# Fourteen modulation sums moved from an output projection to the projections ahead of it, pieces of a step issued in written order, and attention's values read as alternating streams

## The chip, the core and the metric

The kernel runs on one core of a Trainium2 chip. The metric is the device time in microseconds (us) of one execution; less is better. Each kernel is one launch that reads its inputs from device memory (HBM) and writes its output there.

## The reference, cut to what matters

The reference is a decoder trunk of two layers on 512 tokens of width 2048, in fp32. Layer 0 mixes tokens by chunkwise retention with 8 heads, layer 1 by multi-head latent attention with 16 heads. Each layer is modulated by a vector c through a matrix product of its own, and the last lines below are what the moved sums and the values belong to.

```python
c_act = jax.nn.silu(c)
for i in range(DEPTH):                                   # 2 layers
    mod = (c_act @ ada_w[i] + ada_b[i])[:, None, :]      # 2048 -> 3 * 2048
    shift, scale, gate = jnp.split(mod, 3, axis=-1)
    h = rmsnorm(x, norm_g[i]) * (1.0 + scale) + shift
    y = retention_branch(h, ...) if i == 0 else mla_branch(h, ...)
    x = x + gate * y
return rmsnorm(x, final_norm_g)

# retention_branch: proj = h @ w_in (q, k, v, g); rope on q and k; 4 chunks of 128 tokens;
#                   group norm; (silu(g) * y) @ w_out
# mla_branch:       proj = h @ w_in (cq, ckv, k_rope, g); q and k, v from the low ranks; rope;
s = jnp.where(key_pos[None, :] <= qpos[:, None], s, -1e30)
p = jax.nn.softmax(s, axis=-1)
o = jnp.einsum('bhqk,bhkd->bhqd', p, v)                  # the values
#                   (silu(g) * o) @ w_out
```

## The kernel before, in words

Every fp32 matrix product is done on TensorE (PE) as three products of parts: an operand is split into a high part (a cast on ScalarE, ACT) and a low part (the rest, a subtraction on VectorE, DVE), and `mm3` adds high by high, high by low and low by high into one PSUM bank. A weight tile so passes through four hands before PE can finish with it: a DMA brings it, DVE forms sums of its blocks (many projections are done with seven block products in place of eight, which `seven_steps` and `seven_rows_steps` write), ACT casts the high part, DVE makes the low part.

The work is a list of steps. A step has `prepare` (the sums and splits of its weights, on DVE and ACT), `multiply` (on PE), `follow` (what its results need), and pieces of other work that are put beside it (`step.beside["form"]` and others), such as the splits of the rope tables or a head's decayed scores. The step loop issues them in order. A list scheduler then orders the instructions of each engine by their due times; `behind(V_, A_)` around a block says that what is issued in it goes behind what stood there on DVE (`V_`) and ACT (`A_`), so that inside one block the scheduler may reorder and between blocks it may not.

The stages, in order of time: the modulation of layer 0 and the first norm (to about 150 us); the projections of layer 0 (to about 800 us), where heads alternate between `heads_steps(h)` (values and gate, tiles `vg_...`) and `qk_steps(h)` (queries and keys of a head, tiles `qk_...`); the output projection of layer 0 with the retention itself beside it (to about 1370 us, called o1 here, in three rounds of 16 steps, `round_steps`); the input projections of layer 1, among them the gate `g` and the shared rotary key `kr` (to about 1500 us); attention with its up-projections (to about 1890 us); the last output projection.

The modulation of later use (the gate of layer 0 and all of layer 1) isn't done on PE: `later_modulation` loads a 128x1024 piece of the matrix (0.52 MB) and DVE multiplies it with c and sums it in one instruction (tile `mod`, L1194). There are 96 such sums. A step's `rows` says how many of them are fetched with it; they run on DVE a step or two later. `light(block, ...)` gives the numbers of the steps of an o1 round that get one.

Two ways of reading a moving operand occur. `mm3` by default reads with `paired`: elements 0, n/2, 1, n/2+1, ... that is, two streams in turn. The values of attention (`values`, a head's 12 products of 512, 384, 256 and 128 columns) read straight through, with `read=lambda t: t`.

Names that come up again: `x_qk, s_qk, z_qk, y_qk` and `x, s, z, y` are PSUM accumulators of the seven-product scheme; `qk_01e` and `qk_01o` are the even and odd weight tiles of the second step of a `qk_steps`, and `_r` marks the raw tile. `m` are the results of the scheme that DVE adds up at the end of a head. In o1, `o_p` are split weights, `o_h, o_l` the parts of the gated results `yT` (L1369, transposed on PE), `s_0f` to `s_3f` the decayed scores (L1317), `rope_t` the rope (L1265 to L1267). In the gate's stage `h_f` and `sums_f` (L514 to L519) are sums of blocks of the activations, `kr_sum` (L1812) the sum of the two halves of the rotary key, and `kr_sw` its swapped quarters (four copies on ACT, L1818).

## Time and profile before

| what | number |
|---|---|
| median of three runs | 2047.1 us (2046.78 to 2047.33) |
| the profiled execution's own time | 2047.42 us |
| its span | 2045.6 us |
| mean granted TensorE clock | 0.999 of full speed |
| matmuls, share of the span in which PE was busy | 11124, 99% |
| DVE busy | 82% |
| ACT busy | 51% |
| HBM traffic | 418 MB read, 43 MB written |

The span is what the profiler sees of the program on the core; 1.8 us of the execution's own time lie outside of it. A busy engine in the table is one with an instruction in it. PE's matmuls overlap one another, so how much time PE lost is read from the distance between the starts of matmuls, not from the busy share.

### The profile page before, as it was taken

What the parts mean: (1) busy time and instruction counts of PE and PEld (TensorE: products, weight loads), DVE (VectorE), ACT (ScalarE), POOL (GpSimd) and SP (SyncE); (2) the same over time, 40 slices, a digit from 0 to 9 for tenths busy, and PEclk for the clock granted to TensorE, in tenths of its full rate; (3) what the DMA queues carried; (4) which work ended last, traced back from release to release, by engine and by line L of the source; (5) the groups of instructions that cost most, each with busy time, mean ns of one, the idle gap of its engine ahead of it and who ended that gap; (6) DMA issues with size and microseconds to landing.
All of it is one profiled execution on the core that took longest, in us unless ns stands there. A gap on an engine that the chain in (4) does not pass through costs nothing.

```text
span 2045.6 us, 30080 instructions
## 1 busy us (share of the span) xinstructions
PE 2020.9 (99%) x11124; PEld 1807.7 (88%) x11124; DVE 1673.8 (82%) x2506; ACT 1051.9 (51%) x1622; POOL 103.6 (5%) x176
## 2 busy tenths in 40 slices
PE   8999999999999999999999999999999999999998
PEld 6888898999999888888888888899889999999888
DVE  7999888888889889766777878778988788887765
ACT  6765444545454544434444445445446676674444
POOL 1001000000000000000000000010000000000000
PEclk9999999999999999999999999999999999999999
DMA  9985887878787778865757656753467644346644
GB/s 382 406 309 170 274 293 223 288 234 271 254 272 257 240 250 294 267 199 188 243 176 240 223 190 241 273 189 114 160 206 214 199 144 148 120 151 220 232 152 144
DMA packets 230101, 462.95 MB, mean 226 GB/s; under 512 B 20881, under 2 KB 84401, under 8 KB 226369
## 3 DMA queue, kind: packets, MB, share of 16 engines
q1 hardware_dynamic: 217312, 421.07, 62.1%
q0 software_dynamic: 11920, 38.91, 4.9%
q8 instruction: 87, 1.43, 0.3%
q10 hardware_dynamic: 722, 1.06, 0.2%
q14 instruction: 60, 0.49, 0.1%
HBM read 417.96 MB, written 43.00 MB: 225 GB/s over the span
## 4 chain that ended last, share of the span: by engine, by line
PE 72%; DVE 14%; ACT 5%; DMA 5%; issue 3%; SPq 0%; POOL 0%; DVEq 0%; ACTq 0%; POOLq 0%
PE o L1512 5%; PE o L2487 4%; PE x L907 2%; PE s L908 2%; PE s L906 2%; PE y L906 2%; PE y L908 2%; PE x L908 2%; PE y L907 2%; PE s L907 2%; PE x L906 2%; PE x_qk L1007 2%; PE uv L2076 2%; PE s_qk L1007 2%; PE y_qk L1007 2%
## 5 line engine op out<-in xcount | busy, mean ns | idle before, releaser
L1512 PE MATMUL o<-o_h,o_p 128*128 128x512 f32 (+1 forms) x1088 | 311.6, 368 | 0.2 <-DVE o_p L136 0.2
L1512 PEld LDWEIGHTS o<-o_h,o_p 128*128 128x128 f32 x1088 | 201.0, 189 | 25.9 <-DVE o_p L136 0.6
L1512 PE MATMUL o<-o_l,o_p 128*128 128x512 f32 (+1 forms) x544 | 199.8, 367 | 0.4 <-DVE o_l L1390 0.4
L1512 PEld LDWEIGHTS o<-o_l,o_p 128*128 128x128 f32 x544 | 103.0, 189 | 13.7 <-DVE o_l L1390 1.2
L136 DVE TENSOR_TENSOR o_p<-o_r,o_p 128x1024 fp32r<-128x1024 f32 x64 | 78.1, 1222 | 45.1 <-ACT o_p L135 45.1
L2487 PE MATMUL o<-o_h,o_w 128*128 128x512 f32 (+1 forms) x336 | 79.8, 330 | 0.0
L1194 DVE SCALAR_TENSOR_TENSOR mod<-mod,c_odd 128x1024 f32<-128x1024 f32 x56 | 67.3, 1220 | 14.6 <-DMA mod<-in_ada_t_dram 14.6
L135 ACT CAST o_p<-o_r 128x1024 fp32r<-128x1024 f32 x64 | 66.5, 1050 | 17.4 <-DMA o_r<-in_ret_w_out_dram 9.1
L412 DVE SCALAR_TENSOR_TENSOR aw<-aw,c_all 128x2048 f32<-128x2048 f32 (+1 forms) x37 | 73.2, 1997 | 2.0 <-DMA aw<-in_ada_t_dram 2.0
L181 PE MATMUL qk<-hT,qk_p 128*128 128x512 f32 x192 | 73.1, 381 | 1.2 <-ACT g_st L497 1.2
L183 PE MATMUL qk<-hT,qk_p 128*128 128x512 f32 x192 | 73.1, 380 | 0.4 <-DVE qk_p L136 0.4
L182 PE MATMUL qk<-hT,qk_p 128*128 128x512 f32 x192 | 72.8, 379 | 0.0
L2487 PEld LDWEIGHTS o<-o_h,o_w 128*128 128x128 f32 x336 | 57.8, 190 | 4.7
L1356 ACT ACTIVATE yn<-y,nmr,gn_r 128x512 f32<-128x512 f32 x32 | 22.3, 778 | 66.8 <-DVE nmr L1350 66.8
L2487 PE MATMUL o<-o_l,o_w 128*128 128x512 f32 (+1 forms) x168 | 55.4, 329 | 0.0
L135 ACT CAST o_h<-o_in 128x1024 fp32r<-128x1024 f32 x24 | 25.1, 1047 | 55.7 <-PE o L182 36.9
L136 DVE TENSOR_TENSOR o_l<-o_in,o_h 128x1024 fp32r<-128x1024 f32 x24 | 29.3, 1222 | 28.4 <-ACT o_h L135 28.4
L1194 DVE SCALAR_TENSOR_TENSOR mod<-mod,c_bm 128x1024 f32<-128x1024 f32 x40 | 48.7, 1219 | 0.0
L181 PE MATMUL o<-o_h,o_w 128*128 128x512 f32 x128 | 48.7, 381 | 0.0
L182 PE MATMUL o<-o_l,o_w 128*128 128x512 f32 x128 | 48.5, 379 | 0.0
L183 PE MATMUL o<-o_h,o_w 128*128 128x512 f32 x128 | 48.5, 379 | 0.0
L136 DVE TENSOR_TENSOR o_w<-o_w_raw,o_w 128x1024 fp32r<-128x1024 f32 x32 | 38.8, 1219 | 8.5 <-ACT o_w L135 8.4
(1533 smaller groups left out, 6194.4 us busy)
## 6 DMA issues: line engine op xcount, KB each, us to landing
mod<-in_ada_t_dram SPq DMA_DIRECT2D x96, 512.0 KB, 5.7
o_r<-in_ret_w_out_dram SPq DMA_DIRECT2D x64, 512.0 KB, 5.5
aw<-in_ada_t_dram SPq DMA_DIRECT2D x28, 1024.0 KB, 9.7
mod_gate<-in_ada_t_dram SPq DMA_DIRECT2D x32, 512.0 KB, 4.8
o_w_raw<-in_mla_w_out_dram SPq DMA_DIRECT2D x32, 512.0 KB, 4.5
qk_r<-in_ret_w_in_dram SPq DMA_DIRECT2D x48, 256.0 KB, 3.6
qk_r<-qk_d SPq DMA_DIRECT2D x32, 256.0 KB, 6.0
v_r<-v_d SPq DMA_DIRECT2D x32, 256.0 KB, 5.7
```

The lines of the kernel that those rows point to most:

```text
L135: ACT.copy(hi, src)
L136: DVE.tensor_sub(lo, src, hi.bitcast(F32))
L181: PE.matmul(o, lhs[0], read(rhs[0]), start=first and not seeded, stop=False, skip_group_check=seeded)
L182: PE.matmul(o, lhs[0], read(rhs[1]), start=False, stop=False, skip_group_check=seeded)
L183: return PE.matmul(o, lhs[1], read(rhs[0]), start=False, stop=last, skip_group_check=seeded)
L906: PE.matmul(banks[b], a[0], paired(w[0]), start=first, stop=False, skip_group_check=True)
L907: PE.matmul(banks[b], a[0], paired(w[1]), start=False, stop=False, skip_group_check=True)
L908: PE.matmul(banks[b], a[1], paired(w[0]), start=False, stop=True, skip_group_check=True)
L1007: PE.matmul(o, w[wp][:, i, b * P : (b + 1) * P], paired(a[ap]), start=first and i + b + k == 0, stop=k == 2, skip_group_check=True,)
L1194: DVE.scalar_tensor_tensor(out=aw, in0=aw, scalar=1.0, in1=silu_c[j], op0=ALU.mult, op1=ALU.mult, accum_out=row_sums[piece][:, j, b : b + 1],)
L1512: PE.matmul(o, w[i][:, ki, c0 + b * P : c0 + (b + 1) * P], read(a[j]), start=first and i + j == 0, stop=last and i == 1, skip_group_check= ...
L2487: PE.matmul(banks2[b][:, cols], w[0][i][:, 0, b * P : (b + 1) * P], read(o2_moving(w, u, cols)[j]), start=u + i + j == 0, stop=u == KD - 1 ...
```

## The change

It has four parts. (1) Three views are new: `paired_blocks` reads each 128-column block as two streams of 64 in turn, `turned_blocks` and `folded_blocks` undo that in the result. (2) The numbers of sums per step change: in the second half of each head's seven-product steps (`heads_steps`) every step but the first and the last gets one, in `qk_steps` three steps instead of two; that places 14 more sums in the projections. The three o1 rounds get 11, 11 and 12 sums in place of 16 each. (3) `values` reads with `paired_blocks`, and the multiplication that follows reads the result in the turned way. (4) Each piece of `step.beside["form"]` now stands in a block of its own, so that the pieces of a step keep their written order on DVE and ACT.

```diff
+    def paired_blocks(t):
+        return t.rearrange("p (b a n) -> p b n a", a=2, n=P // 2)
+
+    def turned_blocks(t):
+        return t.rearrange("p (b n a) -> p b a n", a=2, n=P // 2)
+
+    def folded_blocks(t):
+        return t.rearrange("p (b a n) -> p b a n", a=2, n=P // 2)
...
-            lambda second, u: int(second and (u % 2 == 1 or (h > 5 and u in (2, 4)))),
+            lambda second, u: int(second and 0 < u < 7),
...
-            f"qk{h}", load_half, hT, sums1, *turns1, finish, lambda second, u: int(second and u < 2),
+            f"qk{h}", load_half, hT, sums1, *turns1, finish, lambda second, u: int(second and u < 3),
...
-        light(block, (0, 0, 2, 3, 4, 6, 6, 7, 9, 9, 11, 11, 12, 13, 13, 15))
+        light(block, (0, 0, 2, 3, 4, 6, 6, 7, 9, 12, 15) + ((13,) if n == 2 else ()))
...
-                    (pt[j][:, 0, o : o + w], pt[j][:, 1, o : o + w]), m == 0, m == NT - 1, read=lambda t: t,
+                    (pt[j][:, 0, o : o + w], pt[j][:, 1, o : o + w]), m == 0, m == NT - 1, read=paired_blocks,
...
-            DVE.tensor_mul(o2, side["o"], side["sg"])
+            DVE.tensor_mul(folded_blocks(o2), turned_blocks(side["o"]), folded_blocks(side["sg"]))
...
-        with behind(V_, A_):
-            for form_ in step.beside["form"]:
+        for form_ in step.beside["form"]:
+            with behind(V_, A_):
                 form_()
```

The change adds nine lines ahead of most of the code, so that L1044 of before is L1053 of the changed kernel.

The first place is DVE where head 1 ends and the `qk_steps` of head 2 begin (tiles `qk_00`, `qk_01`; `m_1_...` are the four results of head 1). Before:

```order
L1044 TENSOR_TENSOR qk_00e<-qk_00e_r,qk_00e 128x1024
L1047 TENSOR_TENSOR qk_00o<-qk_00o_r,qk_00o 128x1024
L1104 TENSOR_TENSOR m_1_0_2162<-m_1_0_2162,y_0_1831 128x512
L1106 TENSOR_TENSOR m_1_0_2120<-m_1_0_2120,y_0_1831 128x512
L1104 TENSOR_TENSOR m_1_1_2164<-m_1_1_2164,y_1_1832 128x512
L1106 TENSOR_TENSOR m_1_1_2122<-m_1_1_2122,y_1_1832 128x512
L1040 TENSOR_TENSOR qk_01e_r<-qk_01e_r 128x2x256
L1042 TENSOR_TENSOR qk_01o_r<-qk_01o_r,qk_01e_r 128x2x256
L1043 TENSOR_TENSOR qk_01o_r<-qk_01o_r 128x2x256
L1044 TENSOR_TENSOR qk_01e<-qk_01e_r,qk_01e 128x1024
L1047 TENSOR_TENSOR qk_01o<-qk_01o_r,qk_01o 128x1024
L1194 SCALAR_TENSOR_TENSOR mod_2_0_11_2351,mod_2_0_c<-mod_2_0_11_2351,c_bm_2156 128x1024
```

And in the changed kernel:

```order
L1053 TENSOR_TENSOR qk_00e<-qk_00e_r,qk_00e 128x1024
L1056 TENSOR_TENSOR qk_00o<-qk_00o_r,qk_00o 128x1024
L1203 SCALAR_TENSOR_TENSOR mod_2_0_21_2325,mod_2_0_c<-mod_2_0_21_2325,c_bm_2156 128x1024
L1113 TENSOR_TENSOR m_1_0_2162<-m_1_0_2162,y_0_1831 128x512
L1115 TENSOR_TENSOR m_1_0_2120<-m_1_0_2120,y_0_1831 128x512
L1113 TENSOR_TENSOR m_1_1_2164<-m_1_1_2164,y_1_1832 128x512
L1115 TENSOR_TENSOR m_1_1_2122<-m_1_1_2122,y_1_1832 128x512
L1049 TENSOR_TENSOR qk_01e_r<-qk_01e_r 128x2x256
L1051 TENSOR_TENSOR qk_01o_r<-qk_01o_r,qk_01e_r 128x2x256
L1052 TENSOR_TENSOR qk_01o_r<-qk_01o_r 128x2x256
L1053 TENSOR_TENSOR qk_01e<-qk_01e_r,qk_01e 128x1024
L1056 TENSOR_TENSOR qk_01o<-qk_01o_r,qk_01o 128x1024
```

A sum now stands ahead of the four results and of the tiles of the second step, and the one behind `qk_01o` is gone from there. On PE, at the second step of the same `qk_steps`, before:

```order
L1007 MATMUL x_qk_2423<-hT_537,qk_01e 128x256 x6
L1007 MATMUL x_qk_2423<-hT_674,qk_01e 128x256 x6
L1007 MATMUL s_qk_2424<-sums_1510,qk_01e 128x256 x6
L1007 MATMUL s_qk_2424<-sums_1555,qk_01e 128x256 x6
L1007 MATMUL z_qk_2425<-hT_554,qk_01o 128x256 x6
```

And in the changed kernel:

```order
L1016 MATMUL x_qk_2430<-hT_537,qk_01e 128x256 x2
L1016 MATMUL s_qk_2431<-sums_1510,qk_01e 128x256 x2
L1016 MATMUL z_qk_2432<-hT_554,qk_01o 128x256
L1016 MATMUL x_qk_2430<-hT_537,qk_01e 128x256 x4
L1016 MATMUL x_qk_2430<-hT_674,qk_01e 128x256 x6
L1016 MATMUL s_qk_2431<-sums_1510,qk_01e 128x256 x4
```

Three products, two of `s_qk` and one of `z_qk`, now stand between the first two of `x_qk` and the third, which is the first that reads the low part of `qk_01e`.

The second place is DVE in an o1 round, where the rope of the next head and the low parts of the gated results meet. Before:

```order
L136 TENSOR_TENSOR o_2_0_2_p<-o_2_0_2_r,o_2_0_2_p 128x1024
L1265 TENSOR_TENSOR rope_0_0_t_10789<-qk_6_r,cos_7826 128x512
L1266 TENSOR_TENSOR rope_0_0_t_10790<-qk_6_r,sin_7828 128x512
L1267 TENSOR_TENSOR rope_0_0_t_10789<-rope_0_0_t_10789,rope_0_0_t_10790 128x512
L1390 SCALAR_TENSOR_TENSOR o_l_0_10777<-yT_0_10749,vcol,o_h_0_10776 128x512
L1390 SCALAR_TENSOR_TENSOR o_l_0_10777<-yT_1_10754,vcol,o_h_0_10776 128x512
L1390 SCALAR_TENSOR_TENSOR o_l_2_10779<-yT_2_10759,vcol,o_h_2_10778 128x512
L1390 SCALAR_TENSOR_TENSOR o_l_2_10779<-yT_3_10764,vcol,o_h_2_10778 128x512
L136 TENSOR_TENSOR qk_0_0p<-rope_0_0_t_10789,qk_0_0p 128x512
```

And in the changed kernel:

```order
L136 TENSOR_TENSOR o_2_0_2_p<-o_2_0_2_r,o_2_0_2_p 128x1024
L1399 SCALAR_TENSOR_TENSOR o_l_0_10789<-yT_0_10761,vcol,o_h_0_10788 128x512
L1399 SCALAR_TENSOR_TENSOR o_l_0_10789<-yT_1_10766,vcol,o_h_0_10788 128x512
L1399 SCALAR_TENSOR_TENSOR o_l_2_10791<-yT_2_10771,vcol,o_h_2_10790 128x512
L1399 SCALAR_TENSOR_TENSOR o_l_2_10791<-yT_3_10776,vcol,o_h_2_10790 128x512
L1274 TENSOR_TENSOR rope_0_0_t_10801<-qk_6_r,cos_7872 128x512
L1275 TENSOR_TENSOR rope_0_0_t_10802<-qk_6_r,sin_7874 128x512
L1276 TENSOR_TENSOR rope_0_0_t_10801<-rope_0_0_t_10801,rope_0_0_t_10802 128x512
L136 TENSOR_TENSOR qk_0_0p<-rope_0_0_t_10801,qk_0_0p 128x512
```

The four low parts moved ahead of the three instructions of the rope.

The third place is DVE in the gate's stage of layer 1, where the rotary key's sum and the activations' sums meet (`g_1_0_p`, `g_1_1_p` are the gate's split weights). Before:

```order
L136 TENSOR_TENSOR g_1_0_p<-g_1_0_r,g_1_0_p 128x1024
L514 TENSOR_TENSOR h_f<-h_2_12499 128x512
L514 TENSOR_TENSOR h_f<-h_3_12503 128x512
L1812 TENSOR_TENSOR kr_sum<-kr_ps,kr_other 128x512
L516 TENSOR_TENSOR sums_f_13044<-h_f 128x256
```

And in the changed kernel:

```order
L136 TENSOR_TENSOR g_1_0_p<-g_1_0_r,g_1_0_p 128x1024
L1821 TENSOR_TENSOR kr_sum<-kr_ps,kr_other 128x512
L523 TENSOR_TENSOR h_f<-h_2_12499 128x512
L523 TENSOR_TENSOR h_f<-h_3_12503 128x512
L525 TENSOR_TENSOR sums_f_13044<-h_f 128x256
```

`kr_sum` moved ahead of the two `h_f`. Eleven rows on, the rotary key's three instructions L1819 to L1821 (L1828 to L1830 of the changed kernel), which stood between the next two `h_f`, stand ahead of both.

## Rows read from the trace of the kernel before

**Rows 1.** The page: busy time, share of the span and instructions of each engine.

```profile
PE 2020.9 (99%) x11124; PEld 1807.7 (88%) x11124; DVE 1673.8 (82%) x2506; ACT 1051.9 (51%) x1622; POOL 103.6 (5%) x176
```

**Rows 2.** Windows: stretch, PE, PEld, DVE, ACT, POOL busy (instructions), PEclk, DMA share, GB/s.

```profile
250.00:800.00 550.00, 549.73 (x3190) 498.56 (x3189) 481.54 (x610) 269.47 (x325) 37.34 (x64) 1.00 0.80 263
...
800.00:1370.00 570.00, 565.37 (x2790) 496.45 (x2789) 437.31 (x697) 253.31 (x378) 22.75 (x35) 1.00 0.66 221
...
1500.00:1890.00 390.00, 390.00 (x2561) 363.85 (x2560) 319.75 (x567) 243.43 (x486) 16.99 (x26) 1.00 0.55 173
```

**Rows 3.** Timeline of DVE at two changes of tile kind: start, us, line, out<-in.

```profile
275.71 1.22 DVE L1044 TENSOR_TENSOR qk_01e<-qk_01e_r,qk_01e 128x1024 fp32r<-128x1024 f32 x1
...
278.12 1.22 DVE L1194 SCALAR_TENSOR_TENSOR mod<-mod,c_bm 128x1024 f32<-128x1024 f32 x1
...
281.32 1.22 DVE L1044 TENSOR_TENSOR qk_02e<-qk_02e_r,qk_02e 128x1024 fp32r<-128x1024 f32 x1
...
309.47 1.29 DVE L1155 TENSOR_TENSOR m_qk<-m_qk,y_qk 128x512 f32<-128x512 f32 x2 [0.17 <-PE y_qk L1007]
...
312.73 1.22 DVE L938 TENSOR_TENSOR vg_01e<-vg_01e_r,vg_01e 128x1024 fp32r<-128x1024 f32 x1
```

**Rows 4.** Timeline of PE at the same places, at a head's start, and in the gate's stage.

```profile
276.90 1.50 PE L1007 MATMUL x_qk<-hT,qk_01e 128*128 128x256 f32 x12
...
282.26 1.71 PE L1007 MATMUL x_qk<-hT,qk_02e 128*128 128x256 f32 x12
...
314.67 0.38 PE L907 MATMUL x<-vg_01e,hT 128*128 128x512 f32 x1
...
796.13 0.38 PE L906 MATMUL x<-vg_02e,hT 128*128 128x512 f32 x1
796.65 0.48 PE L907 MATMUL x<-vg_02e,hT 128*128 128x512 f32 x1
...
1451.10 0.48 PE L183 MATMUL g<-h,g_p 128*128 128x512 f32 x1 [0.27 <-DVE g_p L136]
```

**Rows 5.** Windows: four us at the end of head 6, columns as in rows 2.

```profile
776.00:780.00 4.00, 4.00 (x20) 3.44 (x19) 3.94 (x7) 1.68 (x2) 0.00 (x0) 1.00 1.01 358
```

**Rows 6.** Timeline of DVE in the same stretch.

```profile
776.06 0.69 DVE L947 TENSOR_TENSOR vg_17e_r<-vg_17o_r,vg_17e_r 128x512 f32<-128x512 f32 x1 [0.65 <-DMA vg_17o_r<-in_ret_w_in_dram]
```

**Rows 7.** Waits of PE's weight loads in o1 (800 to 1370): total us, times, longest.

```profile
PEld yT L1369 <- DVE s_3f L1317: 3.1, 3, 1.1
PEld y L182 <- DVE v L136: 3.0, 5, 0.8
PEld o L1512 <- DVE o_l L1390: 1.2, 2, 0.8
```

**Rows 8.** Timeline of DVE ahead of the first wait for `s_3f`.

```profile
1043.97 1.22 DVE L1194 SCALAR_TENSOR_TENSOR mod<-mod,c_odd 128x1024 f32<-128x1024 f32 x1
...
1049.06 0.28 DVE L1317 TENSOR_TENSOR s_3f<-s,dec 128x128 f32<-128x128 f32 x1
```

**Rows 9.** Timeline of DVE in the gate's stage of layer 1.

```profile
1425.02 0.69 DVE L1812 TENSOR_TENSOR kr_sum<-kr_ps,kr_other 128x512 f32<-128x512 f32 x1 [5.28 <-PE g L183]
...
1435.15 0.42 DVE L516 TENSOR_TENSOR sums_f<-h_f 128x256 f32<-128x256 f32 x1
```

**Rows 10.** Timeline of ACT in the same stretch.

```profile
1427.80 2.05 ACT L1756 ACTIVATE sgs<-g 128x512 f32<-128x512 f32 x4
...
1430.81 2.50 ACT L1818 COPY kr_sw<-kr_sum 32x512 f32<-32x512 f32 x4
```

**Rows 11.** Timeline of PE: retention's scores (paired), then attention's values (straight through).

```profile
1038.42 0.38 PE L181 MATMUL s<-qk_0p,qk_0p 128*128 128x512 f32 x1
...
1041.98 0.43 PE L1512 MATMUL o<-o_h,o_p 128*128 128x512 f32 x1
...
1661.27 0.40 PE L181 MATMUL o<-pt,v 128*128 128x512 f32 x1
...
1663.14 1.28 PE L2145 MATMUL pT<-ident,p__15352 128*128 128x128 f32 x10
```

## The prediction, made before the changed kernel ran

> **What bounds the kernel now.** I read the page first: PE is busy for 99% of the span, DVE for 82%, ACT for 51% [rows 1]. So PE is the path almost everywhere, and an instruction on DVE or ACT costs time only where PE stands still for it. The windows by stage show where that is [rows 2]: the projections of layer 0 lose 0.3 us of 550 in busy time, o1 4.6 us of 570, attention nothing (390.00 of 390). A matmul that starts late but overlaps the one before loses time too, so behind the windows I read the starts of matmuls, then the waits of PE's weight loads, then DVE's timeline ahead of each wait.
>
> What such a wait costs is seen where `qk_02e` enters. Its low part begins at 281.32, lasts 1.22 and ends at 282.54 [rows 3]. PE's products of that tile begin at 282.26 and are about 0.11 apart (twelve last 1.50 us in the row of `qk_01e`, twelve of `qk_02e` 1.71), so the third, the first that needs the low part, is due at 282.48 [rows 4]. It is 0.06 short and PE loses 0.21. I price a wait as the shortfall plus 0.15.
>
> **The sums that come: 14 in the projections.** A sum holds DVE for 1.22 us and the next instruction starts 1.14 later [rows 3]. Where DVE has idle time that is free; DVE is busy for 481.5 of 550 us here [rows 2], and 14 sums take 16 us. It isn't free where DVE is back to back, at the end of a head.
>
> Head to `qk_steps` (heads 1 to 4, four places). The order rows show a sum newly ahead of the four results `m` and of `qk_01e`. The low part of `qk_01e` ended at 275.71 + 1.22 = 276.93 and was due at 276.90 + 0.22 = 277.12 [rows 3, 4]: 0.20 to spare. Now it ends at 278.07. PE's order has three other products ahead, three times 0.11, so the due time moves to 277.46. Short by 0.61, price 0.76. The wait of 0.21 at `qk_02e` goes, since the sum that stood ahead of that tile is gone and PE is later. Net 0.55, four times: **+2.2**. (The `z_qk` product moved ahead waits for the high part of `qk_01o`, which moves by the same 1.14; I take the later of the two, not both.)
>
> `qk_steps` to head (heads 2 to 5, four places). The sum now stands ahead of `m_qk`, where DVE was idle for 0.17 [rows 3]; so what follows moves by about 0.9. The low part of `vg_01e` ended at 312.73 + 1.22 = 313.95 and was due at 314.67 [rows 3, 4]: 0.72 to spare. Short by 0.17, price 0.32, four times: **+1.3**.
>
> Heads 5 to 6 and 6 to 7, where no `qk_steps` lies between: PE already stands at the second tile (796.13 to 796.65 where 0.22 is usual) [rows 4]. The sum there moves the wait forward rather than adding one: **+0.2** for both.
>
> Inside the second half every step but the first and the last now has a sum. Head 6 had that partly, and there the DMA queues are full: share 1.01, 358 GB/s, DVE busy 3.94 of 4 us [rows 5]. DVE waits 0.65 there for a weight tile [rows 6], and PE is still busy for 4.00 of 4. Heads 1 to 5 become like this. The sum's load is 0.52 MB, and SP issues it among the weight loads that a step needs next. I allow **+0.3** for all of it; a rival has the rest. Projections: **+4.0**, bounds +1 (the spare times are larger than I read) and +8.
>
> **The sums that go: 14 in o1.** They stood at steps 9, 11, 11, 13 and 13 of each round. At 1043.97 one of them stands ahead of the decayed scores, and `s_3f`, which PE's transposes wait for, comes at 1049.06 [rows 8]. Weight loads of the transposes waited three times, 3.1 us, the longest 1.1 [rows 7]. Taking 1.14 or 2.28 us of DVE's work from ahead of each covers every one of them: about **-3.2** with the weight loads' exposed ends. The written order puts the low parts `o_l` ahead of the rope (second place of the order rows); two waits of 1.2 us in all [rows 7] go, less about 0.15 of each in which the matmul before still ran: **-0.9**. The waits for the low part of v, 3.0 us in five [rows 7], stay for the most part, since a product of the scores' transposes takes the place of the sums: **-0.4**. o1: **-4.5**, bounds -3.0 and -5.0. The displaced sums no longer cover anything: what DVE does in their place is wait.
>
> **The written order in the gate's stage.** `kr_sum` waited 5.28 us for PE and began at 1425.02 [rows 9]. The two `h_f` stood ahead of it in that idle time; now they stand behind it, so the sums of the activations come 1.3 us later (two instructions, 0.66 each). Next late is ACT, in order: it does those sums' casts and then the four copies `sgs` (1427.80) that empty PSUM banks for PE, then the four copies `kr_sw`, 1430.81 to 1433.31, now to 1434.6 [rows 10]. The rope of the key waits for them and now stands ahead of the next two `h_f`: two steps of 0.6 and two `h_f` more, so `sums_f` goes from 1435.15 [rows 9] to 1437.2, **2.05 later**. From here on each step's chain (sums, cast, low part, split weight) is what PE waits for, up to the row at 1451.10 [rows 4]; so PE's time there moves by 2.05, less the three products (0.65) that PE's new order does first: **+1.4**, bounds +0.8 and +2.05.
>
> **The values.** A head's twelve products take 1663.14 - 1661.27 = 1.87 us, read straight through. Retention's scores read the same widths as two streams in turn, two sets of twelve in 1041.98 - 1038.42 = 3.56 us, 1.78 a set, the last weight load's end in it [rows 11]. Sixteen heads by 0.09 to 0.12: -1.4 to -1.9. No row shows streams that lie only 64 elements apart with 512 columns, as these will; the scores' widths, 512 down to 128, with distances of 256 down to 64, are the nearest row. So the bounds are 0 and -1.9, and I take **-1.9**. DVE's product of the result reads PSUM in turn as well; attention's PE waits for nothing [rows 2], so the store behind it hides it.
>
> The rows of the scores speak against a rule, which I name for that. The Trainium skill, "SBUF — State Buffer", section "Specifications (TRN2)", says that a cacheline is 16 bytes, that at least two hits per line are needed for full bandwidth and that each crossing to a new line costs. By it the turn-taking read would cross at every element and be the slower one, where the straight read stays in a line for four. The trace has it the other way round for the distances that it shows.
>
> **The sum.** +4.0 - 4.5 + 1.4 - 1.9 = -1.0, against the profiled execution's own 2047.4: 2046.4. That execution lies 0.3 above the median of the three runs, so I forecast a median of **2046.1**.
>
> **Rivals.** 0.2% (4.1 us) is about what a measurement of this kernel can tell from no change; so faster means below 2043.0, slower above 2051.2.
>
> *Dense heads run late on DMA* (the other side). Heads 1 to 5 each get two more loads, 1.05 MB; at the 358 GB/s of rows 5 that is 2.9 us of the queues. If the queues have no free time in the second half of a head, the last weight tiles come up to 2.9 us late, against the 0.65 that PE didn't feel [rows 6]: up to 2.2 us lost a head, 11 in all. Against it: over the whole stage the share is 0.80 [rows 2], and loads are issued three steps ahead. A middle value, 1.2 a head, adds 6: 2052. It decides from 1.0 a head, that is, tiles 1.65 late.
>
> *The new waits in the projections don't come.* My spare times are 0.20 and 0.72 us, and the order of DVE can absorb a sum if ACT's high part was what held the low parts up. Then +4.0 becomes +0.5, and the time is 2042.6. For it: PE has nearly no loss in that stage now. Against: DVE's rows are without a gap over the twelve instructions concerned.
>
> *The values gain nothing*, since two streams 64 apart meet like a straight read: 2048.0. *They lose*, by the rule of lines: if the 1.9 turned over, 2049.9; the scores speak against it.
>
> That the change doesn't do what it says is excluded by the order rows: the sums, the low parts and the key's sum do stand elsewhere.
>
> **How the numbers follow.** Forecast 0.52 (by its bounds 2044.5 to 2048.5); values gain nothing 0.12; values lose 0.04; dense heads late 0.14; no new waits 0.18. Faster is the fourth, 0.18; slower the dense heads, 0.14; the rest, 0.68, lies within 0.2%. The range goes from 2042.4, which takes in most of the case without new waits, to 2050.6, which takes in the values' cases and the milder half of the dense heads.
>
> **What the changed profile would show.** Right, if PE's third product of `qk_01e` in heads 2 to 5 starts some 0.7 late and `qk_02e` on time; if the transposes of o1 wait for no `s_3f`; if the products with `g_1_2` to `g_1_4` come about 2 us later against the work ahead of them; if a head's values take 1.75 to 1.78 us. Wrong, if DVE's rows at the ends of heads 1 to 5 name a DMA as what they waited for with PE idle behind, if PE's losses in 250 to 800 stay near 1 us, or if the waits of o1 only change their name.

## The result and the profile after

The changed kernel takes 2051.6 us (median of 9 runs, 2051.1 to 2054.5); the kernel before took 2047.45 in the same series (9 runs). The ratio is 1.0022, 95% interval 1.0014 to 1.0031: slower, by 4.2 us, where 2046.1 was forecast and 2050.6 was the upper end of the range. The ratios, here and below, are taken over all runs of a series and differ a little from the ratio of the two medians.

The page of the changed kernel gives the same picture as [rows 1], in a span that is 4.2 us longer (2049.8).

```profile
PE 2020.3 (99%) x11124; PEld 1805.7 (88%) x11124; DVE 1675.4 (82%) x2506; ACT 1051.9 (51%) x1622; POOL 103.4 (5%) x176
```

The windows of the changed kernel, with the columns of [rows 2], put the loss in the projections (PE 544.93 busy in place of 549.73) and a gain in o1 (567.68 in place of 565.37):

```profile
250.00:800.00 550.00, 544.93 (x3160) 492.47 (x3159) 491.19 (x632) 266.83 (x322) 37.32 (x64) 1.00 0.82 273
800.00:1370.00 570.00, 567.68 (x2791) 498.67 (x2790) 426.91 (x671) 254.44 (x378) 22.27 (x34) 1.00 0.63 211
```

To add up what overlapping matmuls hide, I took the starts of six named matmuls from PE's timeline in each trace, and from them the length of each stage: to the first product with `qk_00e` of head 2 (271.55 us in before); to the last product of `x` with `vg_17o` of head 7 (855.89); to the first product of layer 1's gate (1377.91, o1 with the retention); to the first product of the tile `vgc_00e` that follows the gate (1471.74); and from the first to the last product of the values (1661.27 to 1886.13). What lies between or behind these is the same within 0.1 us, but for 0.3 in one kernel. The first column is the length in before, the others the difference to it, in us.

| stage | before | changed | values alone | order alone | sums alone | sums, no loads |
|---|---|---|---|---|---|---|
| start to head 2 | 271.55 | +0.3 | -0.6 | -0.4 | -0.2 | 0.0 |
| heads 2 to 7 | 584.34 | +7.1 | +0.2 | 0.0 | +7.7 | +4.3 |
| o1 and retention | 522.02 | -3.5 | -0.1 | +7.3 | -5.1 | -2.8 |
| gate of layer 1 | 93.83 | +2.2 | 0.0 | +2.2 | 0.0 | +2.2 |
| values, first to last | 224.86 | -1.9 | -1.9 | 0.0 | 0.0 | -1.9 |

Each column is one execution. Where nothing is changed, the first row still differs by half a us, the heads differ by up to 0.6, and o1 by 1.3 (two more executions of the changed kernel's o1 are below); the gate and the values agree within 0.1.

PE's own waits say where. In 250 to 870 us of the changed kernel (total us, times, longest; the same view of before is empty there):

```profile
PE z_qk L1016 <- ACT qk_01o L1055: 2.6, 4, 0.7
PE x L916 <- DVE vg_17o L957: 2.1, 2, 1.3
PE z L915 <- ACT vg_01o L949: 0.6, 2, 0.3
PE x L916 <- DVE vg_16o L957: 0.3, 1, 0.3
```

The first line is the head-to-`qk_steps` term, four times as forecast. DVE, PE and ACT at the first of the four:

```profile
271.60 1.22 DVE L1203 SCALAR_TENSOR_TENSOR mod<-mod,c_bm 128x1024 f32<-128x1024 f32 x1
...
277.19 1.22 DVE L1053 TENSOR_TENSOR qk_01e<-qk_01e_r,qk_01e 128x1024 fp32r<-128x1024 f32 x1
```

```profile
277.45 0.39 PE L1016 MATMUL s_qk<-sums,qk_01e 128*128 128x256 f32 x2
278.47 0.38 PE L1016 MATMUL z_qk<-hT,qk_01o 128*128 128x256 f32 x1 [0.62 <-ACT qk_01o L1055]
```

```profile
277.36 1.05 ACT L1055 CAST qk_01o<-qk_01o_r 128x1024 fp32r<-128x1024 f32 x1 [0.42 <-DVE qk_01o_r L1052]
```

The sum now runs at 271.60, ahead of the results; `qk_01e` comes at 277.19, where it came at 275.71 [rows 3]; 0.3 of that is the delay of the whole program, the rest the sum. PE goes through its first four products and then stands for the high part of `qk_01o`, which the same sum delayed and which ends together with the low part of `qk_01e`, at 278.41.

The second line of the waits was not forecast at that place. DVE and PE where head 6 ends:

```profile
780.10 0.69 DVE L956 TENSOR_TENSOR vg_17e_r<-vg_17o_r,vg_17e_r 128x512 f32<-128x512 f32 x1 [0.19 <-DMA vg_17o_r<-in_ret_w_in_dram]
...
782.91 1.23 DVE L1203 SCALAR_TENSOR_TENSOR mod<-mod,c_bm 128x1024 f32<-128x1024 f32 x1 [0.25 <-DMA mod<-in_ada_t_dram]
...
786.05 0.69 DVE L943 TENSOR_TENSOR vg_00e_r<-vg_00e_r 128x512 f32<-128x512 f32 x1 [1.91 <-DMA vg_00e_r<-in_ret_w_in_dram]
786.66 1.22 DVE L957 TENSOR_TENSOR vg_17o<-vg_17o_r,vg_17o 128x1024 fp32r<-128x1024 f32 x1
```

```profile
787.93 0.48 PE L916 MATMUL x<-vg_17o,hT 128*128 128x512 f32 x1 [1.31 <-DVE vg_17o L957]
```

The raw tile of `vg_17o` was there at 780.1. Its low part stands on DVE behind the first instruction on a tile of the *next* head, `vg_00e`, and that tile's load is 1.9 us late. So PE waits 1.3 us for a load whose tile it doesn't need yet. At the end of head 7 it is a sum's own load:

```profile
859.92 1.23 DVE L1203 SCALAR_TENSOR_TENSOR mod<-mod,c_bm 128x1024 f32<-128x1024 f32 x1 [1.16 <-DMA mod<-in_ada_t_dram]
861.07 0.08 DVE L1203 DVE_READ_ACCUMULATOR mod<-mod,c_bm 128x1 f32 x1
861.07 1.22 DVE L957 TENSOR_TENSOR vg_17o<-vg_17o_r,vg_17o 128x1024 fp32r<-128x1024 f32 x1
```

In o1 the transposes of [rows 7] and the low parts `o_l` are gone from the waits, and waits for v are left: first PE's (900 to 1375 us), then those of its weight loads (800 to 1370, the view of [rows 7], where v stood at 3.0 us in five).

```profile
PE y L191 <- DVE v L136: 0.8, 3, 0.3
PE y L190 <- ACT v L135: 0.6, 1, 0.6
PE x_sums L1240 <- DVE x L1485: 0.6, 1, 0.6
```

```profile
PEld y L191 <- DVE v L136: 3.6, 8, 0.6
PEld y L190 <- ACT v L135: 1.6, 3, 1.0
```

In the gate's stage the two rows that answer to [rows 9 and 10], and PE behind them:

```profile
1428.92 0.69 DVE L1821 TENSOR_TENSOR kr_sum<-kr_ps,kr_other 128x512 f32<-128x512 f32 x1 [6.49 <-PE g L192]
1429.53 1.28 DVE L523 TENSOR_TENSOR h_f<-h 128x512 f32<-128x512 f32 x2
...
1439.89 0.69 DVE L523 TENSOR_TENSOR h_f<-h 128x512 f32<-128x512 f32 x1
```

```profile
1433.02 2.05 ACT L1765 ACTIVATE sgs<-g 128x512 f32<-128x512 f32 x4
```

```profile
1433.66 0.48 PE L190 MATMUL g<-h,g_p 128*128 128x512 f32 x1 [0.86 <-ACT sgs L1765]
```

DVE idles for 6.5 us with two `h_f` that it could do, because `kr_sum` stands first. The copies `sgs` begin 5.2 us later than in before, 3.9 of which is the whole program's delay at this point and 1.3 the new order's; PE waits for the bank.

And the values: twelve products from the first row to the second, 1.75 us, where 1.87 were read in [rows 11].

```profile
1667.34 0.38 PE L190 MATMUL o<-pt,v 128*128 128x512 f32 x1
...
1669.09 0.63 PE L2154 MATMUL pT<-ident,p__15352 128*128 128x128 f32 x4
```

### The profile page after: what moved, and what is told of

Same layout as the page of the kernel before. It is cut to its first block, busy times and chain, and to the rows that moved or that the text cites. A ratio compares the mean times of both kernels' runs of the same rounds, so it can differ in the third digit from the quotient of the medians.

```text
span 2049.8 us, 30079 instructions
## 1 busy us (share of the span) xinstructions
PE 2020.3 (99%) x11124; PEld 1805.7 (88%) x11124; DVE 1675.4 (82%) x2506; ACT 1051.9 (51%) x1622; POOL 103.4 (5%) x176
## 4 chain that ended last, share of the span: by engine, by line
PE 48%; issue 29%; DVE 9%; DMA 6%; ACT 5%; POOL 2%; SPq 0%; DVEq 0%; POOLq 0%; ACTq 0%
PE o L1521 12%; PE o L2496 4%; PE uv L2085 2%; PE o L191 2%; PE o L192 2%; PE o L190 2%; DMA qk_r<-qk_d 1%; PE y_g L1016 1%; PE s_g L1016 1%; PE x_g L1016 1%; DVE aw L421 1%; PE uq L192 1%; PE uq L191 1%; PE uq L190 1%; PE a L2113 1%
## 5 line engine op out<-in xcount | busy, mean ns | idle before, releaser
L1203 DVE SCALAR_TENSOR_TENSOR mod<-mod,c_bm 128x1024 f32<-128x1024 f32 x54 | 65.8, 1219 | 1.4 <-DMA mod<-in_ada_t_dram 1.4
L1203 DVE SCALAR_TENSOR_TENSOR mod<-mod,c_odd 128x1024 f32<-128x1024 f32 x42 | 50.9, 1220 | 13.0 <-DMA mod<-in_ada_t_dram 13.0
```

What stands on the lines that cost most here:

```text
L1203: DVE.scalar_tensor_tensor(out=aw, in0=aw, scalar=1.0, in1=silu_c[j], op0=ALU.mult, op1=ALU.mult, accum_out=row_sums[piece][:, j, b : b + 1],)
```

## The experiments

Medians are given with those of the kernel before in the same series, ratios with their 95% intervals.

**One part at a time.** The three parts of the change were each put alone on the kernel before: the diff's lines on the values, on the pieces' order, and on the sums.

`values_alone`:

```diff
-                    (pt[j][:, 0, o : o + w], pt[j][:, 1, o : o + w]), m == 0, m == NT - 1, read=lambda t: t,
+                    (pt[j][:, 0, o : o + w], pt[j][:, 1, o : o + w]), m == 0, m == NT - 1, read=paired_blocks,
...
-            DVE.tensor_mul(o2, side["o"], side["sg"])
+            DVE.tensor_mul(folded_blocks(o2), turned_blocks(side["o"]), folded_blocks(side["sg"]))
```

> Only the reading of the values is changed. In the changed kernel a head's twelve products took about 1.76 us in place of 1.87. Theory (the parts add up): 16 times 0.11 is 1.7 us less than before, no other matmul start moves, ratio about 0.9992. Rival (the turned reading of the result, or the parts' interplay, takes it back): no difference to before.

Measured: 2045.63, before 2047.34; ratio 0.9992 (0.9983 to 1.0001). The interval just reaches 1, but the stage from the first to the last product of the values is shorter by 1.91 us and nothing else is. The theory holds.

`order_alone`:

```diff
-        with behind(V_, A_):
-            for form_ in step.beside["form"]:
+        for form_ in step.beside["form"]:
+            with behind(V_, A_):
                 form_()
```

> Only the written order of a step's pieces. Theory (the sums in the projections carry the loss): the gate's stage loses about 2 us, the low parts ahead of the rope give back 0.9, sum +1 to +1.5, ratio 1.0005 to 1.0007. Rival (the written order carries it): +4 or more, ratio 1.002.

Measured: 2055.71 (5 runs), before 2047.34; ratio 1.0038 (1.0025 to 1.0050). The theory's size holds for the gate, 2.2 us as in the changed kernel, and falls for o1: 7.3 us are lost there, where a gain of 0.9 had been forecast. Standing alone, this is the most harmful part, with twice the 4 us that the rival named as the least. PE's waits in o1 (870 to 1376 us) of this kernel, first three lines, and DVE ahead of a wait for v of 1.3 us:

```profile
PE yT L1369 <- DVE s_3f L1317: 2.5, 3, 0.8
PE y L181 <- ACT v L135: 2.5, 2, 1.3
PE o L1512 <- DVE o_p L136: 1.3, 3, 0.5
```

```profile
1124.77 1.23 DVE L1194 SCALAR_TENSOR_TENSOR mod<-mod,c_odd 128x1024 f32<-128x1024 f32 x1 [2.37 <-DMA mod<-in_ada_t_dram]
...
1130.50 0.29 DVE L136 TENSOR_TENSOR sT<-s_3f,sT 128x128 fp32r<-128x128 f32 x1 [0.36 <-ACT sT L135]
1130.71 0.69 DVE L1265 TENSOR_TENSOR rope_t<-qk_r,cos 128x512 f32<-128x512 f32 x1
```

The same stretch of DVE in before:

```profile
1119.19 1.23 DVE L1194 SCALAR_TENSOR_TENSOR mod<-mod,c_odd 128x1024 f32<-128x1024 f32 x1 [1.97 <-DMA mod<-in_ada_t_dram]
...
1125.49 0.68 DVE L1265 TENSOR_TENSOR rope_t<-qk_r,cos 128x512 f32<-128x512 f32 x1
1126.09 0.28 DVE L136 TENSOR_TENSOR sT<-s_3f,sT 128x128 fp32r<-128x128 f32 x1
```

The transposes' waits stay, since the sums do, and the wait for v on ACT is new. The sum's wait of 2.37 us for its load isn't: DVE waits for sums' loads in seven places of o1 in both kernels, 15.1 us in all here and 14.6 in before. What differs is the rope. It starts only when the last piece of the scores is done, whose low part waits 0.36 for ACT; in before the rope's first instruction ran at 1125.49, inside that hole, ahead of the low part at 1126.09. DVE's waits for the parts of the scores (870 to 1376 us) show it for all of o1, first before, then this kernel; the changed kernel has 2.9 in eight too, and the kernel with the sums alone 1.5 in four.

```profile
DVE sT L136 <- ACT sT L135: 1.5, 4, 0.4
```

```profile
DVE sT L136 <- ACT sT L135: 2.9, 8, 0.4
```

ACT casts v behind the rope's result, so v arrives late at PE. Between the starts of its matmuls PE loses 5.0 us at v in o1 where it lost 1.7, which is 3.3 of the 7.3 us. Another 1.4 are lost at `qk_p` near 875 us, 1.4 more at `o_p` and 0.9 more at the first of the transposes; these weren't followed to their causes. The low parts `o_l`, which cost PE 0.6 us in before, are waited for no more.

`sums_alone`:

```diff
-            lambda second, u: int(second and (u % 2 == 1 or (h > 5 and u in (2, 4)))),
+            lambda second, u: int(second and 0 < u < 7),
...
-            f"qk{h}", load_half, hT, sums1, *turns1, finish, lambda second, u: int(second and u < 2),
+            f"qk{h}", load_half, hT, sums1, *turns1, finish, lambda second, u: int(second and u < 3),
...
-        light(block, (0, 0, 2, 3, 4, 6, 6, 7, 9, 9, 11, 11, 12, 13, 13, 15))
+        light(block, (0, 0, 2, 3, 4, 6, 6, 7, 9, 12, 15) + ((13,) if n == 2 else ()))
```

> Only the 14 sums moved. Theory (the sums carry the loss): +7 to +8 us before the end of the last head (about 860 us), 2 to 3 back in the output projection of layer 0, ratio 1.002 to 1.003. Rival (the written order carries it): within 1 us of before.

Measured: 2050.16, before 2047.34; ratio 1.0012 (1.0003 to 1.0021). The heads bear out the theory's size, +7.7; o1 gives 5.1 back in place of 2 to 3, so the ratio lies below the expected one. In PE's waits in o1 (870 to 1376 us) neither the transposes nor `o_l` appear, with the pieces in the scheduler's free order, and its weight loads wait for neither:

```profile
PE x_sums L1231 <- DVE x L1476: 0.6, 1, 0.6
PE y L182 <- DVE v L136: 0.2, 1, 0.2
```

So the sums' absence gives the whole gain of o1, that of the low parts too. The rest of the changed kernel's difference to this one is -1.9 of the values, +2.2 in the gate and +1.6 in o1: the written order costs 3.8 us in the profiled execution of the changed kernel. The 1.6 is a lower end. Two kernels below have the changed kernel's o1 instruction for instruction (`key_last`, `last_heads`) and stand at -2.2 and -1.9 there, with waits for `o_p` and `qk_p` added that come and go between executions; with the same sums and a free order o1 is at -4.9 to -5.3 in three kernels (`sums_alone`, `order_late`, `spread`).

**Loads or DVE's time.** `sums_no_loads`, the changed kernel; all 54 sums of the projections, not the 14 new ones alone, read a tile that is there anyway:

```diff
-            nc.sync.dma_start(
-                aw, ada_t[i, r0 : r0 + P, j * 1024 : (j + 1) * 1024].rearrange("p (a n) -> p a n", a=2)
-            )
+            if tag != "bw":
+                nc.sync.dma_start(
+                    aw, ada_t[i, r0 : r0 + P, j * 1024 : (j + 1) * 1024].rearrange("p (a n) -> p a n", a=2)
+                )
...
-                    out=aw, in0=aw, scalar=1.0, in1=silu_c[j], op0=ALU.mult, op1=ALU.mult,
+                    out=aw, in0=aw if tag != "bw" else silu_c[j], scalar=1.0, in1=silu_c[j], op0=ALU.mult, op1=ALU.mult,
```

> The changed kernel, with the sums of the projections computed from a tile that is already there: their loads are left out, their DVE instructions stay, and the modulation that they make is not the reference's. Theory (two causes: DVE's time at the starts, late loads at the ends of heads 1, 6 and 7): the waits of 0.5, 1.5 and 0.9 us at the ends of heads go, the 0.8 us at the second tile of each qk step stays; 2.5 to 3 us less than the changed kernel, about 2048.7. Rival (DVE's time alone): as the changed kernel, 2051.6. Rival (the loads alone): all of the projections' loss goes, 7 us less, about 2044.5.

Measured: 2049.73, before 2047.34; ratio 1.0011 (1.0002 to 1.0020). In the heads +4.3 is left of +7.1. PE's waits in 250 to 870 us and DVE where head 6 ends:

```profile
PE z_qk L1016 <- ACT qk_01o L1055: 2.6, 4, 0.7
PE z L915 <- ACT vg_01o L949: 0.6, 2, 0.3
```

```profile
783.27 0.69 DVE L943 TENSOR_TENSOR vg_00e_r<-vg_00e_r 128x512 f32<-128x512 f32 x1
783.87 1.22 DVE L957 TENSOR_TENSOR vg_17o<-vg_17o_r,vg_17o 128x1024 fp32r<-128x1024 f32 x1
```

The waits at the tiles `vg_16o` and `vg_17o` are gone and `vg_00e_r` waits for nothing; the others stay to the tenth. So 2.8 us of the heads' loss are late loads, and 4.3 are DVE's time. The starts of PE's products in the changed kernel say the same: 2.6 us are lost at the two `vg_17o`. The median is 1 us above what was expected, while the heads' difference is the one that was named; o1, which has the changed kernel's program, is at -2.8 here.

**Undoing one place each.** `last_heads`, the changed kernel with the sixth sum of heads 6 and 7 at its old step:

```diff
-            lambda second, u: int(second and 0 < u < 7),
+            lambda second, u: int(second and (0 < u < 7 if h < 6 else u in (1, 2, 3, 4, 5, 7))),
```

> The changed kernel, with the sums of heads 6 and 7 at the steps that they had before (the last of the six one step later). Theory (the sixth sum's load and instruction ahead of the last weight tile make that tile late): the waits of 1.5 and 0.9 us at the last tile of heads 6 and 7 go, the two of 0.48 at the second tile of the next head become the 0.3 of before; about 2.5 us less than the changed kernel, 2049.1. Rival (14 more loads fill the queues, wherever the last one stands): no difference, 2051.6.

Measured: 2051.96, before 2047.85; ratio 1.0017 (1.0008 to 1.0026): no gain over the changed kernel. In the heads +6.1 in place of +7.1. The wait at the end of head 7 went; that at the end of head 6 stayed (1.4 us) and one of 0.4 at the end of head 5 came. The rival is right for head 6: there the loads are late wherever the last sum stands. The 1.0 us that the heads gain doesn't reach the median; in the profiled execution o1 is at -1.9 in place of -3.5, though its program is the same.

`order_late`, the changed kernel with the written order from the gate's stage on only:

```diff
-        for form_ in step.beside["form"]:
-            with behind(V_, A_):
-                form_()
+        forms = step.beside["form"]
+        for group in ([f] for f in forms) if i >= n_l2 else (forms,):
+            with behind(V_, A_):
+                for form_ in group:
+                    form_()
```

> The changed kernel, with the written order only from the gate's stage on and the scheduler's free order in the output projection of layer 0. Theory (written order costs there too, since a piece's rope can no longer fill the hole in which the scores' cast is waited for): the waits of 0.4 to 0.75 us for v go to what they are with the sums moved alone; 1 to 2 us less than the changed kernel, about 2050. Rival (the low parts ahead of the rope gain, as forecast): 0.9 more, 2052.5.

Measured: 2050.94, before 2047.85; ratio 1.0013 (1.0004 to 1.0021). O1 and the retention are at -5.3 to before, like the sums alone, 1.8 better than the changed kernel; 1 us of that is lost again in late tiles at the ends of heads, where the program is the same. With the sums moved, the forecast gain of the low parts ahead of the rope isn't there.

`key_last`, the changed kernel with the two pieces of the rotary key appended behind the activations' sums of their steps:

```diff
-    ga[7].beside["form"].append(kr_sum)
...
-    g1[0].beside["form"].append(kr_rope)
...
         step.beside["form"].append(lambda u=u: form_sums(u, h2, sums2, staged2, more2, apart=True))
+    ga[7].beside["form"].append(kr_sum)
+    g1[0].beside["form"].append(kr_rope)
```

> The changed kernel, with the rotary key's two pieces written behind the activations' sums of their steps. Theory (the key's place ahead of the sums makes the gate's wait): the 1.0 us at the first bank, the 0.4 and 0.5 behind it go to what they were before or less; 2.3 us less than the changed kernel, about 2049.3. Rival (the fixed order as such holds DVE, whatever comes first): less than 0.5 us.

Measured: 2051.41, before 2047.85; ratio 1.0017 (1.0009 to 1.0026). The gate's stage is at +0.8 in place of +2.2. PE's waits from 1376 to 1485 us, first line:

```profile
PE g L192 <- DVE g_p L136: 1.3, 3, 0.8
```

No wait for `sgs` is left, so the key's place made that one; but in this order too the chain of the sums is late, 0.8 us more than in before. The median doesn't show the 1.3 us. In the profiled execution o1 takes them back: with the changed kernel's program it is at -2.2 in place of -3.5. One wait there (870 to 1376 us) isn't among those of the changed kernel. Besides, the runs spread from 2049.7 to 2053.5.

```profile
PE o L1521 <- DVE o_p L136: 0.4, 1, 0.4
```

**Another place for the same sums.** `spread`, the kernel before with the values' reading, the fewer sums in o1, the third sum in each `qk_steps`, no written order, and the sixth sum of each head at its last step:

```diff
-            lambda second, u: int(second and (u % 2 == 1 or (h > 5 and u in (2, 4)))),
+            lambda second, u: int(second and u in (1, 2, 3, 4, 5, 7)),
```

> The kernel before, with the values' reading and the 14 sums moved, but the sixth sum of every head at its last step in place of the sixth, and no written order. Theory (what costs is the sum that stands ahead of the next tile's low part, not its number): the 0.8 us at the second tile of each qk step go, and the ends of heads 6 and 7 as in before; of the projections' loss about 1 us stays, the output projection of layer 0 gives 4 back, the values 1.7; about 2043. Rival (14 more sums fill DVE and the queues): the loss moves to other tiles, 2047 to 2049.

Measured: 2044.23, before 2047.85; ratio 0.9987 (0.9978 to 0.9995). Stages: -0.1, +3.5, -4.9, 0.0, -1.9 in the table's order. The four waits of 0.8 us are gone with as many sums in each head as in the changed kernel, so it was their place. At the end of head 6 the theory didn't hold: the one wait left in 250 to 870 us is there, and DVE's row ahead of it names the next head's tile again:

```profile
PE x L916 <- DVE vg_17o L957: 1.2, 1, 1.2
```

```profile
783.25 0.69 DVE L943 TENSOR_TENSOR vg_00e_r<-vg_00e_r 128x512 f32<-128x512 f32 x1 [1.50 <-DMA vg_00e_r<-in_ret_w_in_dram]
```

`spread_five` gives head 5 its four sums back and o1 the two others (its 12 steps are 0, 0, 2, 3, 4, 6, 6, 7, 9, 12, 13, 15 in every round):

```diff
-            lambda second, u: int(second and u in (1, 2, 3, 4, 5, 7)),
+            lambda second, u: int(second and u in ((1, 3, 5, 7) if h == 5 else (1, 2, 3, 4, 5, 7))),
```

> The spread kernel with four sums in head 5 as before (its two others at step 13 of the first two rounds of the output projection of layer 0). Theory (heads 5 and 6 follow each other without a qk step between, and 12 sums' loads put the queues behind, so that the first tile of head 7 and with it the last of head 6 comes late): the wait of 1.4 us at the last tile of head 6 goes; the stage of the heads takes 1.4 to 2 us less than in the spread kernel, and the median is about 2042.5. Rival (one sum too many at the end of head 6 itself): no difference in that stage.

Measured: 2043.41, before 2047.61; ratio 0.9980 (0.9971 to 0.9988). The heads' stage goes from +3.5 to +1.6 and the wait at the end of head 6 is gone: the backlog was made in head 5. The load of `vg_00e` that DVE waits for there shows it: issued at 775.09 in `spread`, it was used at 783.25, as soon as it had landed, 8.2 us later; issued at 775.53 in `spread_five`, it landed at 782.08, after 6.6 us. The median is 0.9 above what was expected; in the profiled execution 0.7 us went to a late tile at the end of head 1 (below).

`spread_more` also takes the third sum of each `qk_steps` back (their rule is `u < 2` again) and puts those four into o1, at step 14 of each round and step 1 of the second:

```diff
-        light(block, (0, 0, 2, 3, 4, 6, 6, 7, 9, 12, 13, 15))
+        light(block, (0, 0, 2, 3, 4, 6, 6, 7, 9, 12, 13, 14, 15) + ((1,) if n == 1 else ()))
```

> As the kernel with four sums in head 5, but with two sums in each qk step's head as before; the four others stand at step 14 of the three rounds and at step 1 of the second. Theory (each third sum of a qk costs a wait of 0.2 at the next head's second tile, three times): 0.7 us less in the heads, nothing more in the output projection of layer 0, about 2041.8. Rival (the output projection's steps have no room for a thirteenth sum either): its waits come back, 1 us or more for each round, 2044 and more.

Measured: 2042.62 (2042.11 to 2043.09), before 2047.61; ratio 0.9974 (0.9963 to 0.9984). Heads +0.9 in place of +1.6, the 0.7 that the theory named, and o1 -4.2 in place of -4.4. It is 9.0 us below the changed kernel (which ran in another series) and 5.0 below before; 6 of the 14 sums are back in o1 and most of its gain is still there. One wait is left in 250 to 870 us:

```profile
PE x L916 <- DVE vg_17o L957: 0.2, 1, 0.2
```

`places` moves none of the sums out of o1, only to other steps of it (with the values' reading, no written order):

```diff
-        light(block, (0, 0, 2, 3, 4, 6, 6, 7, 9, 9, 11, 11, 12, 13, 13, 15))
+        light(block, (0, 0, 1, 2, 3, 4, 5, 6, 6, 7, 9, 10, 12, 13, 14, 15))
```

> The kernel before with the values' reading, no sum moved out of the output projection of layer 0 and no written order; of the 16 sums of a round the second of step 9, the two of step 11 and the second of step 13 stand at steps 1, 5, 10 and 14. Theory (the place of a sum decides, not how many a round has): the transposes' waits for the decayed scores go and nothing is lost in the heads; the output projection of layer 0 takes 4 us less than before, median about 2041.8. Rival (a round has no room for 16 sums; its DVE must be relieved): waits of 1 us or more come up elsewhere in each round, median 2044 to 2046.

Measured: 2044.19, before 2048.0; ratio 0.9982 (0.9973 to 0.9991). It lies between the two theories: o1 is at -1.8. The transposes' waits are gone; waits for v stand in their place (870 to 1376 us, first two lines):

```profile
PE y L191 <- DVE v L136: 1.6, 5, 0.4
PE y L190 <- ACT v L135: 0.8, 3, 0.4
```

So the place of a sum within the round is worth about 1.8 us, and that 8 of the sums go, as in `spread_more`, 2.4 more. Both come from one execution each, where o1 can differ by 1.3, and the round's other steps differ a little too. I didn't try which of the four new steps costs what.

## Why the prediction was wrong, step by step

By the stages the change costs 4.2 us where a gain of 1.0 was forecast. Of these 5.2 us, 3.4 are the projections, 1.0 is o1 and 0.8 the gate. The steps that failed are the allowance of 0.3 for full queues, which measured 2.8, and the gain of 0.9 that the written order was to bring in o1, where it costs 1.6 or more. The range was also narrower than the working: the bounds of the four terms, added up, reach from 2042.0 to 2054.2, and the time lies within them.

**The values, -1.9: right** in mechanism and size (-1.91, measured alone and in the changed kernel). Two streams 64 elements apart read like those of the scores, whose products of 512 columns start every 216 ns too. By the rule of the Trainium skill that was weighed there ("SBUF — State Buffer", "Specifications (TRN2)") the reading would have become slower; the traces differ, and the measurement decides.

**Head to `qk_steps`, +2.2: right place, somewhat small.** The four waits are there, at `qk_01` of heads 2 to 5, 0.79, 0.78, 0.79 and 0.91 us between starts beyond the usual and 0.11 more at the next start, against 0.76 forecast. The 0.21 at `qk_02e`, four times in before, is gone as forecast. In all about +3.0.

**`qk_steps` to head, +1.3: nearly held**, three waits of 0.22 to 0.24, with 0.11 more at the next start, in place of four of 0.32: +1.0. **Heads 5 to 6 and 6 to 7, +0.2: held** (0.48 each in place of 0.30).

**The allowance of 0.3 for full queues: the term that was mis-sized most.** It measured 2.8 us in heads 2 to 7, and 0.5 at the end of head 1. I had taken head 6 of before as what a dense head looks like: DVE waits 0.65 for a tile and PE feels nothing. Two things were left out: that heads 5 and 6 stand next to each other without a `qk_steps` between, so that a denser head 5 hands its backlog to head 6; and that on DVE the last low part of a head stands behind the first instruction on the next head's tile, or behind a sum, so that PE pays for *their* loads. The rival of late loads had the mechanism and was given 0.14; its places were wrong (heads 1 to 5 in place of 1, 6 and 7). That its 2052 came near the time is luck: it put 6 us on late loads, which cost 3.3.

**O1, -4.5: one step failed in its sign.** That the sums' leaving would free the transposes was right, and so was its size: they cost PE 3.4 us between starts in before and nothing in the changed kernel, against 3.2 forecast. That "the written order puts the low parts ahead of the rope" and gains 0.9 is the step that failed. The order does free the low parts, which cost PE 0.6 us in before; but the sums' leaving frees them too, so there was nothing left to gain, and the written order costs 1.6 us or more in o1 with the sums moved and 7.3 where they are not. I had read only the place in the order rows at which it helps. The piece of the decayed scores ends with a wait of 0.36 for ACT; a free order fills that with the rope's first instruction, a fixed one doesn't, and v is cast behind the rope. So the 0.4 that was to go at v came back as a loss: PE lost 1.7 us there in before, 1.5 with the sums alone and 2.7 in the changed kernel.

**The gate, +1.4: right mechanism, 2.2 measured**, above the upper bound of 2.05. PE's first wait, 1.0 us at the bank that `sgs` empties, was in the working; with the chain behind it PE lost 1.4 us more between starts up to 1458 us than in before, the size forecast. The three products that PE's new order does first were taken off the sum of the delays; the wait for `sgs` at the end of the stage (0.9 where it had been 0.24) was not put on.

In all: heads +7.1 and 0.3 ahead of them where +4.0 stood, o1 -3.5 where -4.5 stood, gate +2.2 where +1.4 stood, values as forecast; +4.2 in place of -1.0.

## What to carry to other kernels

A filler instruction on an engine is priced by what stands behind it in that engine's order, not by its duration against the mean idle time: the same sums in the heads cost 7.7 us or 3.5 by the step at which the sixth stands. Where work with a load is added, look at the last instruction of a stage that PE still needs, and at the tile whose load is waited for by the instruction *ahead* of it. And when code fixes an order, read every place at which the free order had filled a hole, not only the one that the change was seen to improve.

## What the runs showed of the hardware that was not expected

The last tiles of a head land late by different amounts in executions of the same instructions: up to the end of head 1 the changed kernel, `key_last`, `last_heads` and `order_late` are one program, instruction for instruction, and PE lost 0.48, 0.12, under 0.12 and 0.96 us there at `vg_16o`. The runs of kernels with dense heads also lie further apart (the changed kernel 2051.1 to 2054.5 in 9 runs, before 2046.5 to 2048.0 in 9, the one with six of the sums back in o1 2042.1 to 2043.1 in 8). That the late tiles make this difference isn't shown, since one execution of each kernel was profiled. A difference of 1 us in the gate or the values is seen in the stage's own length and not in the median; in o1 one execution can't tell it either.

And the reading of a moving operand: 512 columns start every 216 ns when read as two streams 64 elements apart, where they took 229 to 241 read straight through; by 128 columns there is nothing left to gain (58 to 60 and 111 to 115 ns in both).
